# Two-layer attention trunk: last chunk of v moved in the source, one tile more and one exponential buffer fewer

## The chip, the cores and the metric

The kernel runs on one core of one Trainium2 chip. The metric is the device time of one execution in microseconds (us); lower is better. TensorE (PE) multiplies matrices, VectorE (DVE), ScalarE (ACT) and GpSimd (POOL) work on elements, and SyncE (SP) issues most transfers.

## The reference

The input x is 512 positions by 1024 features in float32. There are two layers, each with a mixer and a gated FFN, both with RMS norms ahead and residual sums behind. Layer 0 is stick-breaking attention with 16 heads. Layer 1 is differential attention with 8 heads:

```
q, k, v = split(h @ w_in, 3)          # q, k: 8 heads x 2 maps x 64; v: 8 heads x 128
q, k = rms_norm(q, q_g), rms_norm(k, k_g)       # then rotation of 16 of 64 features
a = softmax(q1 k1) - lam * softmax(q2 k2)       # visible: key chunk <= query chunk (64)
o = rms_norm(a @ v, sub_g) * (1 - lam_init)
x = x + o @ w_out
x = x + (silu(g @ w_gate) * (g @ w_up)) @ w_down    # g = rms_norm(x)
```

## The kernel before

Activations lie transposed, as eight tiles x of 128 features by 512 positions. For accuracy each operand is split into a high and a low part, and each product is three matmuls (mm3, lines 221 to 223). The normalised input h of a mixer is 16 tiles of the tag "t" in the pool hp, a high and a low one for each 128 features. The outputs of the heads (og) take tiles of the same tag, two for each head in layer 1 and two for each pair of heads in layer 0. HP is the number of these tiles, 25. The low part of pair 4 in layer 0, written in line 547, is the 26th tile of the tag in source order, and h still has a reader after it, the last q and k of the layer.

A planner orders the instructions before the kernel runs. It goes by a priority, the place in the source, and by its own estimate of when things are ready; each engine then works through its list in order. Functions under `ahead` (stacks, weights, banks, head_out) are lifted by 200 places. Everything else keeps its place: the filler, that is the projections of later chunks and of the output, which is meant to fill PE between the steps of attention. Each tile is taken from a pool by its tag; a tag has a fixed number of buffers, and the tile waits for a free one.

Layer 1 runs through heads 0 to 7. A chunk c is the pair of heads 2c and 2c + 1. Chunk 0 is projected first. For chunks 1 to 3 two generators are queued in the order qk 1, v 1, qk 2, v 2, qk 3, v 3:

- qk_steps projects q and k for four groups of 128 positions. A group is two steps; at its end line 784 copies the sums to qk_nat, and lines 786 and 787 square and sum them (a tile of the tag tmp each). After the eighth step comes what is left: the reciprocal root of the sums (line 794, then rsqrt, lines 143 to 149, with tiles rs_u and rs_t), the multiplication by it (line 797), and the rotation on GpSimd (lines 814 to 817, two tmp tiles).
- v_steps projects v, one step for each group of positions, with copies in lines 763 and 764.

A head does the following (attend): the weights for the last group of queries, `after()`, a fill, the next weights and two banks of transposes, a fill, `middle()`, weights, a bank and a fill, and again weights, a bank and a fill. A fill pulls as many steps from the queue as `counts` says for this head and place. `after()` is head_out of the head before: it copies the product with v (line 882), transposes and squares it (line 893, a tmp tile), takes the reciprocal root (lines 143 to 149, again rs_u and rs_t), scales, and writes the output to og (lines 918 and 919). `middle()` stacks q and k for the next head (lines 316, 317, 313, 314; the copies of k by line 336 on GpSimd's queue), and for an odd head it first flushes the queue until the next chunk's qk generator is finished. weights() takes scores (lines 342, 343), maxima (841) and exponentials (842) into e1 and e2 and combines them in e1 (854). The bank (368) transposes e1, lines 371 and 372 split it. Before its product with v a head flushes the v generator of its chunk; head 6 then queues out_first, the first half of the output projection (adds in line 289). out_second is the other half (302).

Of the kernel before, what the change touches and what calls it, by code (L numbers as in the profile page):

```python
# [12 lines left out]
F32 = mybir.dt.float32  # L13
# [8 lines left out]
P = 128  # L22
S = 512
# [9 lines left out]
RSQRT_MAGIC = float(0x5F3759DF)  # L33
AHEAD = 200
TCK = dict(schedule_with_timeline_sim=True)
HP = 25
WB = 5
THIRDS = ((0, 8), (8, 8), (16, 6))
TWO_PI_A = 6.28125
# [5 lines left out]
def trunk(  # L45
# [30 lines left out]
    xp = ctx.enter_context(tc.tile_pool(name="xp", bufs=1))  # L76
    hp = ctx.enter_context(tc.tile_pool(name="hp", bufs=HP))
    wp = ctx.enter_context(tc.tile_pool(name="wp", bufs=WB))
# [203 lines left out]
    def out_first(layer, og):  # L282
        for g in range(4):
            w = out_load(layer, 0, g)
            for mi in range(2):
                m = g * 2 + mi
                ps = mm.tile([P, S], F32, tag="mm", name="ps_o")
                out_mms(ps, w, og, range(4), mi, 0, 3)
                V.tensor_tensor(x[m], x[m], ps, op=ALU.add)
                yield  # L290
# [48 lines left out]
    def scores(ps, q2, k2, e, qt):  # L339
        n = max(2, qt + 1) * P  # L340
        qs = slice(qt * P, (qt + 1) * P)
        T.matmul(ps[:, :n], q2[:, e, qs], k2[:, 0, e, :n], start=True, stop=False)
        T.matmul(ps[:, :n], q2[:, e, qs], k2[:, 1, e, :n], start=False, stop=True)
# [391 lines left out]
    def diff_layer(norm, nxt):  # L735
        h = norm.h
        with ExitStack() as st:
# [3 lines left out]
            at = st.enter_context(tc.tile_pool(name="at1", bufs=2))  # L741
# [89 lines left out]
            @ahead  # L831
            def weights(q2, k2, ss, qt):
                n = (qt + 1) * P
                nm = sm.tile([P, 2], F32, tag="nm", name="nm")
                e1 = at.tile([P, S], F32, tag="e1", bufs=5, name="e1")
                e2 = at.tile([P, S], F32, tag="e2", name="e2")
                for e, o in ((0, e1), (1, e2)):
                    ps = scp.tile([P, S], F32, tag="sc", name="sc")
                    scores(ps, q2, k2, e, qt)
                    V.memset(ps[0:64, n - 64 : n], NEG)  # L840
                    V.reduce_max(nm[:, e : e + 1], ps[:, :n], axis=AX.X, negate=True)
                    A.activation(
                        o[:, :n],
                        ps[:, :n],
                        AF.Exp,
                        bias=nm[:, e : e + 1],
                        accum_out=ss[:, e, qt : qt + 1],
                    )
                c = sm.tile([P, 2], F32, tag="c", name="c")
                V.reciprocal(c[:, 0:1], ss[:, 1, qt : qt + 1])  # L850
                V.tensor_scalar(
                    c[:, 1:2], ss[:, 0, qt : qt + 1], nlam, c[:, 0:1], op0=ALU.mult, op1=ALU.mult
                )
                V.scalar_tensor_tensor(
                    e1[:, :n], e2[:, :n], c[:, 1:2], e1[:, :n], op0=ALU.mult, op1=ALU.add
                )
                return e1

            def head(hh, q2, k2, v, after, middle, steps, before):
                ss = sm.tile([P, 2, TT], F32, tag="s12", name="s12")  # L860
                attend(tpp, wts, lambda qt: weights(q2, k2, ss, qt), after, middle, steps)
                before()
                v = v()
                av = avp.tile([P, S], F32, tag="av", name="av")
                hs = slice(hh * P, (hh + 1) * P)
                with tc.high_priority(AHEAD):
                    for kt in range(TT):
                        n, hi, lo = wt_chunk(wts, kt)
                        mm3(
                            av[:, :n],  # L870
                            (v[0][:, kt, hs], v[1][:, kt, hs]),
                            (hi, lo),
                            kt == 0,
                            kt == TT - 1,
                        )
                return av, ss
# [59 lines left out]
                gens["v", c] = v_steps(c, vs)  # L936
                fillers.extend((gens["qk", c], gens["v", c]))
            last = out_first(1, og)
            counts = ((3, 3, 3, 3), (0, 0, 0, 0)) * 3 + ((1, 1, 1, 1), (1, 1, 1, 1))
            for hd in range(8):  # L940
                hh = hd % 2
                c = hd // 2
# [32 lines left out]
    assert not todo  # L975
    n3 = Norm(gf, KT, True, False)
    diff_layer(n2, n3)
    ffn(1, n3, store)

# [72 lines left out]
```

## Time and profile before

| | us |
|---|---|
| median of 3 runs | 1258.3 |
| their range | 1256.72 to 1261.17 |
| profiled execution | 1261.58 |
| its span, first to last instruction | 1259.8 |
| PE busy | 1226.6 |
| DVE busy | 735.3 |

The span is what the trace covers; the time around it is 1.8 us. Layer 0's mixer ends near 260 us, its FFN near 630, layer 1's mixer near 890, and the rest is the second FFN.

### The profile page before, as it was taken

To read this page: it belongs to the slowest core of one execution; us is meant where nothing else is said; L and a number is where in the kernel's file an instruction comes from. 1 tells how busy PE (TensorE), PEld (TensorE's weight loads), DVE (VectorE), ACT (ScalarE), POOL (GpSimd) and SP (SyncE) were. 2 spreads that over 40 slices of the span, in tenths; PEclk is the share of its full clock that TensorE was granted. 3 is DMA by queue.
4 is the path that set the end of the run, shared out by engine and by line. 5 is a ranking of instruction groups with operands and counts; after the bars stand their busy time and mean duration, and the time that the engine had idled before them with its cause. 6 is when DMAs were issued, how large, how long until landed. Compare 5 with 4: busy or idle time off the path is not lost.

```text
span 1259.8 us, 16064 instructions
## 1 busy us (share of the span) xinstructions
PE 1226.6 (97%) x5974; PEld 1023.5 (81%) x5974; DVE 735.3 (58%) x1382; ACT 565.2 (45%) x963; POOL 125.3 (10%) x181
## 2 busy tenths in 40 slices
PE   7899999999999999999999999987999999999998
PEld 6788988878888888888888898766788888888886
DVE  6468788586556555455634686885764344443442
ACT  7687888454334333334424455463543123222320
POOL 2111112041101001111010102100300000000000
PEclk9899999999999999999999999989999999999999
DMA  7955848337767777767736364421333323332322
GB/s 211 219 124 134 197 95 211 69 130 258 245 220 255 248 251 234 247 229 226 278 146 215 97 217 138 164 67 47 105 101 100 100 85 100 100 97 87 97 75 80
DMA packets 58478, 198.40 MB, mean 157 GB/s; under 512 B 8288, under 2 KB 9312, under 8 KB 58400
## 3 DMA queue, kind: packets, MB, share of 16 engines
q1 hardware_dynamic: 41760, 138.90, 34.5%
q0 software_dynamic: 16208, 57.94, 16.5%
q8 instruction: 47, 0.77, 0.2%
q10 hardware_dynamic: 432, 0.53, 0.1%
q14 instruction: 31, 0.25, 0.1%
HBM read 153.31 MB, written 35.65 MB: 150 GB/s over the span
## 4 chain that ended last, share of the span: by engine, by line
PE 90%; DVE 5%; DMA 3%; ACT 2%; issue 1%; SPq 0%; DVEq 0%; ACTq 0%
PE ps_d L223 7%; PE ps_d L222 7%; PE ps_d L221 7%; PE ps_g L222 6%; PE ps_u L223 6%; PE ps_u L222 6%; PE ps_g L223 6%; PE ps_u L221 6%; PE ps_g L221 6%; PE ps_nat L221 4%; PE ps_nat L222 4%; PE ps_nat L223 4%; PE ps_o L221 2%; PE tp L368 2%; PE ps_o L222 2%; PE ps_o L223 2%
## 5 line engine op out<-in xcount | busy, mean ns | idle before, releaser
L110 ACT ACTIVATE whi<-wraw 128x1024 fp32r<-128x1024 f32 (+1 forms) x138 | 140.6, 1033 | 358.9 <-PE ps_d L222 80.5
L111 DVE TENSOR_TENSOR wlo<-wraw,whi 128x1024 fp32r<-128x1024 f32 (+1 forms) x138 | 166.6, 1208 | 101.9 <-ACT whi L110 52.2
L222 PE MATMUL ps_g<-hlo,whi 128*128 128x512 f32 x352 | 138.0, 392 | 1.5 <-DVE hlo L163 1.5
L222 PE MATMUL ps_d<-alo,whi 128*128 128x512 f32 x352 | 138.9, 396 | 0.0
L223 PE MATMUL ps_d<-ahi,wlo 128*128 128x512 f32 x352 | 138.9, 396 | 0.0
L221 PE MATMUL ps_d<-ahi,whi 128*128 128x512 f32 x352 | 138.7, 396 | 0.0
L221 PE MATMUL ps_u<-hhi,whi 128*128 128x512 f32 x352 | 137.2, 390 | 0.5 <-DVE x L302 0.5
L221 PE MATMUL ps_g<-hhi,whi 128*128 128x512 f32 x352 | 137.6, 391 | 0.0
L223 PE MATMUL ps_g<-hhi,wlo 128*128 128x512 f32 x352 | 137.0, 389 | 0.0
L222 PE MATMUL ps_u<-hlo,whi 128*128 128x512 f32 x352 | 137.0, 389 | 0.0
L223 PE MATMUL ps_u<-hhi,wlo 128*128 128x512 f32 x352 | 136.9, 389 | 0.0
L221 PE MATMUL ps_nat<-whi,hhi 128*128 128x256 f32 (+1 forms) x384 | 125.2, 327 | 0.3 <-DVE v L445 0.2
L223 PE MATMUL ps_nat<-whi,hlo 128*128 128x256 f32 (+1 forms) x384 | 124.2, 324 | 0.0
L222 PE MATMUL ps_nat<-wlo,hhi 128*128 128x256 f32 (+1 forms) x384 | 123.7, 323 | 0.0
L620 DVE TENSOR_TENSOR x<-x,ps_d 128x512 f32<-128x512 f32 x48 | 32.7, 684 | 89.5 <-PE ps_d L223 89.5
L222 PEld LDWEIGHTS ps_g<-hlo,whi 128*128 128x128 f32 x352 | 66.1, 188 | 17.2 <-DVE hlo L163 3.2
L221 PEld LDWEIGHTS ps_nat<-whi,hhi 128*128 128x128 f32 x384 | 73.9, 193 | 7.4 <-DVE v L445 1.0
L222 PEld LDWEIGHTS ps_d<-alo,whi 128*128 128x128 f32 x352 | 66.1, 188 | 16.1
L223 PEld LDWEIGHTS ps_d<-ahi,wlo 128*128 128x128 f32 x352 | 66.1, 188 | 16.0
L221 PEld LDWEIGHTS ps_d<-ahi,whi 128*128 128x128 f32 x352 | 66.1, 188 | 15.9
L221 PEld LDWEIGHTS ps_u<-hhi,whi 128*128 128x128 f32 x352 | 66.1, 188 | 14.9 <-DVE x L302 1.3
L223 PEld LDWEIGHTS ps_nat<-whi,hlo 128*128 128x128 f32 x384 | 73.8, 192 | 5.3
(201 smaller groups left out, 2353.7 us busy)
## 6 DMA issues: line engine op xcount, KB each, us to landing
wraw<-in_wgu SPq DMA_DIRECT2D x88, 512.0 KB, 3.5
wraw<-in_wd SPq DMA_DIRECT2D x32, 512.0 KB, 3.6
praw<-in_wqk SPq DMA_DIRECT2D x16, 512.0 KB, 5.8
kept_wqk<-whi POOLq DMA_DIRECT2D x16, 512.0 KB, 5.4
kept_wqk<-wlo POOLq DMA_DIRECT2D x16, 512.0 KB, 6.3
whi<-kept_wqk SPq DMA_DIRECT2D x16, 512.0 KB, 6.1
wlo<-kept_wqk SPq DMA_DIRECT2D x16, 512.0 KB, 5.5
k<-k POOLq DMA_DIRECT2D x30, 256.0 KB, 3.8
```

What stands on the lines that cost most here:

```text
L110: A.activation(hi[:, :cols], raw[:, :cols], AF.Copy)
L111: V.tensor_tensor(lo[:, :cols], raw[:, :cols], hi.bitcast(F32)[:, :cols], op=ALU.subtract)
L221: T.matmul(ps, lh[0], rh[0], start=first, stop=False)
L222: T.matmul(ps, lh[0], rh[1], start=False, stop=False)
L223: T.matmul(ps, lh[1], rh[0], start=False, stop=last)
L368: T.transpose(tp[:, o : o + P], w[qt][:, kt * P : (kt + 1) * P], ident)
L620: V.tensor_tensor(x[m], x[m], ps, op=ALU.add)
```

## The change

Three edits. HP goes from 25 to 26. The tag e1 of the exponentials has 4 buffers in place of 5. In `counts`, the third pair of rows (heads 4 and 5) goes from three steps a fill to two, and the last pair (heads 6 and 7) still pulls one step a fill. So head 4 pulls the eight steps of qk 3 alone; what follows its eighth step is pulled by the flush in the middle of head 5, and the four steps of v 3 by the four fills of head 6, ahead of out_first.

```diff
-HP = 25
+HP = 26
...
-                e1 = at.tile([P, S], F32, tag="e1", bufs=5, name="e1")
+                e1 = at.tile([P, S], F32, tag="e1", bufs=4, name="e1")
...
-            counts = ((3, 3, 3, 3), (0, 0, 0, 0)) * 3 + ((1, 1, 1, 1), (1, 1, 1, 1))
+            counts = ((3, 3, 3, 3), (0, 0, 0, 0)) * 2 + ((2, 2, 2, 2), (0, 0, 0, 0)) + ((1, 1, 1, 1), (1, 1, 1, 1))
```

## Rows read from the trace of the kernel before

**Rows 1.** Busy shares on the page: engine, busy us (share), instructions.

```profile
PE 1226.6 (97%) x5974; PEld 1023.5 (81%) x5974; DVE 735.3 (58%) x1382; ACT 565.2 (45%) x963; POOL 125.3 (10%) x181
```

**Rows 2.** Stretches: length, busy PE, PEld, DVE, ACT, POOL, clock, DMA share, GB/s.

```profile
800.00:830.00 30.00, 28.09 (x139) 22.89 (x137) 22.46 (x66) 12.84 (x38) 5.71 (x10) 0.94 0.35 116
830.00:870.00 40.00, 33.28 (x169) 26.19 (x167) 29.75 (x109) 21.31 (x65) 1.18 (x2) 0.91 0.13 32
870.00:890.00 20.00, 14.90 (x57) 11.34 (x55) 10.66 (x24) 8.50 (x19) 1.54 (x2) 0.83 0.26 74
```

**Rows 3.** Timeline of GpSimd, 800 to 832: start, duration, engine, line, out<-in.

```profile
803.78 0.45 POOL L814 TENSOR_TENSOR rope<-qk_nat,rot 128x128 f32<-128x128 f32 x1 [14.85 <-DVE qk_nat L797]
...
806.80 1.47 POOL L817 TENSOR_TENSOR qk_nat<-rope 128x256 f32<-128x256 f32 x2
826.96 0.60 POOL L336 DMA_DIRECT2D k<-k  x1 [18.68 <-DVE c L850]
828.72 0.61 POOL L336 DMA_DIRECT2D k<-k  x1 [1.16 <-DVE rs_t L148]
```

**Rows 4.** Timeline of PE: head 4's last transpose, scores of head 6, head 6's last bank.

```profile
813.24 0.27 PE L368 MATMUL tp<-ident,e 128*128 128x128 f32 x1
...
830.16 0.47 PE L342 MATMUL sc<-k,q 128*128 128x512 f32 x1
...
831.76 0.47 PE L342 MATMUL sc<-k,q 128*128 128x512 f32 x1 [0.47 <-DMA k<-k]
...
846.73 0.90 PE L368 MATMUL tp<-ident,e 128*128 128x128 f32 x3 [0.31 <-DVE wt_lo L372]
```

**Rows 5.** Stretches, the matmuls into ps_nat alone: length, busy PE, clock, DMA share, GB/s.

```profile
780.00:800.00 20.00, 10.99 (x81) 1.00 0.83 273
800.00:830.00 30.00, 0.00 (x0) 0.94 0.35 116
```

**Rows 6.** Timeline of ScalarE: copies and squares of chunks 2 and 3.

```profile
729.52 0.69 ACT L784 ACTIVATE qk_nat<-ps_nat,rstd 128x512 f32<-128x512 f32 x1 [0.27 <-PE ps_nat L223]
...
741.53 0.37 ACT L893 ACTIVATE o_sq<-tn,rs 128x128 f32<-128x128 f32 x1
...
741.87 1.16 ACT L786 ACTIVATE qk_sq<-qk_nat 128x512 f32<-128x512 f32 x2
...
776.87 0.69 ACT L784 ACTIVATE qk_nat<-ps_nat,rstd 128x512 f32<-128x512 f32 x1 [3.10 <-PE ps_nat L223]
...
789.37 0.39 ACT L893 ACTIVATE o_sq<-tn,rs 128x128 f32<-128x128 f32 x1
...
789.71 1.18 ACT L786 ACTIVATE qk_sq<-qk_nat 128x512 f32<-128x512 f32 x2
```

**Rows 7.** Timeline of VectorE: ending of chunk 3, head 4's last weights, head 4's root.

```profile
796.05 0.17 DVE L143 TENSOR_SCALAR rs_u<-qk_ss 128x32 int32<-128x32 int32 x1
...
801.34 2.29 DVE L797 TENSOR_TENSOR qk_nat<-qk_nat,rs_u 128x2048 f32<-128x2048 f32 x1
...
807.32 0.36 DVE L854 SCALAR_TENSOR_TENSOR e<-e,c,e 128x128 f32<-128x128 f32 x1
...
826.58 0.15 DVE L143 TENSOR_SCALAR rs_u<-o_ss 128x4 int32<-128x4 int32 x1
```

**Rows 8.** Timeline of ScalarE: stacks of heads 5 and 6, product of head 5, exponential.

```profile
778.58 0.68 ACT L316 ACTIVATE q<-tqk,gqT 64x512 fp32r<-64x512 f32 x1 [0.53 <-PE tqk L827]
...
825.26 0.58 ACT L313 ACTIVATE k<-tqk 64x512 fp32r<-64x512 f32 x1
...
835.69 0.59 ACT L882 ACTIVATE wraw<-av 128x512 f32<-128x512 f32 x1
...
845.98 0.68 ACT L842 ACTIVATE e<-sc,nm 128x512 f32<-128x512 f32 x1
```

**Rows 9.** Timeline of ScalarE and VectorE in layer 0: output of pair 4.

```profile
185.36 0.64 ACT L546 ACTIVATE ohi<-o 128x512 fp32r<-128x512 f32 x1
...
194.59 0.67 DVE L547 TENSOR_TENSOR olo<-o,ohi 128x512 fp32r<-128x512 f32 x1
```

## The prediction, made before the changed kernel ran

> **What bounds the kernel now.** I read the busy shares first. TensorE (PE) is busy 97% of the span [rows 1], so over the whole kernel only about 33 us are not matmul time. The table by stretches then shows where part of these lie in layer 1: from 800 to 890 us PE is busy 28.09 of 30, 33.28 of 40 and 14.90 of 20 us, while VectorE (DVE) has 22.46, 29.75 and 10.66 [rows 2]. That is 13.7 us without a matmul in 90, and the mean granted clock falls to 0.94, 0.91 and 0.83 of full speed, a mix of the 1.2 and 2.4 GHz levels [rows 2]. In this end of the attention little is left to fill PE with, and a chain sets the time: stacks of q and k, scores, exponentials, weights, output of heads 5, 6 and 7. The timelines then show what holds head 6. Its two k transfers are issued on GpSimd's queue at 826.96 and 828.72, its first scores run at 830.16, and the second ones, at 831.76, name the transfer as what they waited for [rows 3, 4]. So head 6's start is bound by its stacks, these by the last chunk of q and k (its normalisation and rotation, called its ending here), and the end of the layer, with the FFN behind it, by heads 6 and 7.
>
> **What the change does to v.** v3, the last chunk of v, is 96 matmuls. Projections of q, k and v take 10.99 us of PE between 780 and 800 and nothing from 800 to 830 [rows 5]. So v3, traced in head 4, is done by 800, though its first reader is head 6's product with v. The planner does not place filler where the source yields it, but once PE is free and the data are there. The change traces v3 in head 6: still behind the last q and k chunk, still ahead of out_first, its four weight loads still ahead of out_first's on the SyncE queue, and attention still ahead of it by the same priority of 200. Nothing that it reads or writes comes later, so I expect v3 to run before 800 as now: price 0, and its copies (0.5 us each on ScalarE and DVE) stay where they are. If it did move, its 10.99 us could fill at most the 13.7 us of gaps; that is a rival below.
>
> **What it does to the ending of qk3.** This edit I price. With (3,3,3,3) head 4 pulled twelve steps: eight of qk3, then its ending, then v3. With (2,2,2,2) it pulls the eight alone. The ending is then traced by the flush in head 5's middle, after head 5 has called head_out for head 4. It uses the tags rs_u, rs_t and tmp, and so does head_out. The trace shows that tiles of one tag are granted in source order, whoever is ready first. The squares of chunk 2 had all their data by 730.2; they ran at 741.87, right behind the last output square of head 1 (741.53), which stands just ahead of them in the source. Those of chunk 3 had theirs by 777.6 and ran at 789.71, behind head 3's last one (789.37) [rows 6]. ScalarE sat idle for 3.10 us before the fourth copy of chunk 3, with squares of earlier copies outstanding [rows 6]. So the ending must now wait until head_out of head 4 has taken its root tiles: 826.58 in this trace, where today the ending's own root starts at 796.05 [rows 7]. Attention of heads 4 and 5 goes on meanwhile on DVE; behind the ending wait the rotation and, on GpSimd's queue, the k transfers of heads 6 and 7, and nothing else.
>
> **The sum.** From the ending's root to head 6's first scores it takes 34.1 us today (796.05 to 830.16): 5.3 for the root, 2.3 for the multiplication, 4.6 for the rotation, then stacks and transfer [rows 3, 4, 7].
> - Upper bound: the gate stays at 826.58 and the path takes 34.1 again. Head 6 starts at 860.7, 30.5 late.
> - Lower bound: head 4 ends sooner, since the ending no longer stands ahead of its last exponentials on DVE. That is 2.29 + 11 x 0.17 = 4.2 us. PE also let head 4's last transposed weights wait from 807.68 to 813.24, 5.6 us [rows 4, 7]. Without both the gate opens at 816.8. The shortest path is a root of 1.9 (11 x 0.17), 2.3, 4.6, q in 3.4 (transposes 0.6, four copies of 0.7, as that at 778.58), k transposes 0.6, and 4.9 from the first k copy to the scores (825.26 to 830.16): 17.7 us [rows 3, 4, 7, 8]. Head 6 starts at 834.5, 4.3 late.
> - My value: the gate at 819.6 (all of the 4.2, half of the 5.6) and a path of 24.0, nearer to the short end, because the 34.1 holds waits behind filler on PE, and PE has gaps by then [rows 2]. Head 6 starts at 843.6, 13.4 late.
>
> Not all of this reaches the end. After head 6's first scores head 5 still used the engines for 5.5 us, until its product was copied out at 835.69 [rows 4, 8]; starting late, head 6 runs alone. I take back 5 of that (0 to 5.5). This leaves 8.4, between 0 and 30. More idle PE may cost more at the lower clock level, as in the three stretches [rows 2]; the upper bound holds that.
>
> **The buffers.** One exponential buffer fewer: a head's four weights are live until its last bank is transposed, so the next head's first exponential must follow the first of those transposes. Head 7's ran at 845.98; the transposes of head 6 began at 846.73 and take 0.3 each, so it would come 1.1 us later [rows 4, 8]. On head 7's path that is 0 to 1.1; I take 0.6. Up to head 3 full PE covers it; without that cover each head would pay up to the same 1.1. One tile more for h and outputs: in layer 0 the low part of pair 4 came at 194.59, 9.2 us after its high part at 185.36 [rows 9]. Counted in the source it is the 26th tile of its tag and waited for an h tile. With 26 it comes at once, but its reader is the second half of the projection, after the last head: 0. In layer 1 head 4's output comes past 826.58, after v3 has freed h: 0 too.
>
> A rule would have this otherwise. The Trainium skill, Perfetto Trace Analysis, section Optimization Strategy under Identifying Performance Opportunities, says that a gap repeating on the engine that should be saturated can mean too little memory for the next tile. By it the h tile could be worth those 9.2 us, and the sum would fall to 1258. The trace bears it out only in part: the late tile is there, but it is a DVE result on which PE does not wait.
>
> Sum: 8.4 + 0.6 = 9.0 us on the profiled 1261.6, which lies 3.3 above the median of the runs. That gives 1270.6 there and **1267** as a median.
>
> **Rivals.**
> - The ending comes late but is hidden, or grants are looser than I read them. At the lower bound the 4.3 is eaten by the 5 taken back: 1258. For it: 4.8 us pass today between the rotation's end (808.27) and the next transposes of q (near 813), which can shrink. Against: head 6 starts the moment its k lands.
> - On the other side, the ending leaves DVE to head 4. If head 4 finishes so early that the gate opens before 812.5 (830.16 less 17.7), head 6 starts sooner than today and the 4.2 us saved on head 4's chain are kept: 1254. This needs 14.1 us from head 4, of which the rows show 9.8.
> - v3 does move into head 6 and half of its 10.99 us fill gaps: 1258.3 - 5.5 = 1253. Against: filler runs when ready [rows 5].
> - The h tile lifts a stall in layer 0: 1258.3 - 9.2 = 1249. Against: its only readers come after the last head.
>
> **How the numbers follow.** Late ending, slower: 0.60, its own range 1262 to 1282. Hidden or no change: 0.21. Early gate 0.10, v3 moved 0.06, h tile 0.03. A measurement of this kernel can tell about 0.3%, 3.8 us, from no change; so faster 0.19, same 0.21, slower 0.60. The range 1254 to 1279 leaves out the far side of the faster rivals and the top of the upper bound, under 2 in 10 together.
>
> **What the next profile would show.** Right: qk3's multiplication only after head 4's root has begun, the rotation ending past 824, head 6's first scores past 835 with a PE gap ahead of them; v3 still before 800; head 7's first exponential behind head 6's last transposes; in layer 0 pair 4's low part some 1 us behind its high part. Wrong: that multiplication still near 801, which would mean that grants are not in source order; v3 matmuls past 830; head 4's product copied out before 808.

## The result, and the profile after

The changed kernel takes 1267.44 us (median of four executions, 1266.91 to 1268.62) against 1258.43 us for the kernel before (four executions). The ratio is 1.0077, 95% interval 1.0063 to 1.0092: slower by 9.0 us, outside the 0.3% that the prediction takes as the least it can tell. The forecast was 1267.0 us, slower. The profiled execution took 1268.62 us, 7.0 over that of before.

The page's busy shares of the changed kernel have the same count of instructions on every engine as [rows 1]; PE is busy 3.6 us longer:

```profile
PE 1230.2 (97%) x5974; PEld 1024.7 (81%) x5974; DVE 738.2 (58%) x1382; ACT 565.3 (45%) x963; POOL 125.2 (10%) x181
```

The three stretches of [rows 2], in the changed kernel:

```profile
800.00:830.00 30.00, 26.71 (x130) 22.06 (x128) 21.06 (x73) 9.52 (x32) 0.04 (x1) 0.96 0.29 104
830.00:870.00 40.00, 28.33 (x101) 20.24 (x99) 26.16 (x79) 19.54 (x53) 6.81 (x12) 0.65 0.12 26
870.00:890.00 20.00, 18.26 (x90) 14.62 (x91) 11.37 (x45) 7.62 (x26) 0.00 (x0) 1.00 0.21 65
```

The middle stretch is the one that changed: 101 matmuls where [rows 2] have 169, 11.7 us without any, and a mean granted clock of 0.65, so most of it at 1.2 GHz. GpSimd's work (POOL) has moved out of the first stretch into it.

The stretches of the matmuls into ps_nat, as in [rows 5]: v3 is still done before 800 (its last matmul starts at 789.88).

```profile
780.00:800.00 20.00, 7.25 (x56) 6.96 (x56) 1.91 (x4) 1.90 (x4) 1.00 0.64 183
800.00:830.00 30.00, 0.00 (x0) 0.00 (x0) 0.00 (x0) 0.00 (x0) 0.96 0.29 104
```

VectorE's timeline after, against [rows 7]. The ending's root (128x32) starts in the slot behind the root of head 4 (128x4), at 824.26 where it was 796.05:

```profile
824.10 0.16 DVE L143 TENSOR_SCALAR rs_u<-o_ss 128x4 int32<-128x4 int32 x1
...
824.26 0.15 DVE L143 TENSOR_SCALAR rs_u<-qk_ss 128x32 int32<-128x32 int32 x1
...
827.49 2.29 DVE L797 TENSOR_TENSOR qk_nat<-qk_nat,rs_u 128x2048 f32<-128x2048 f32 x1
```

GpSimd's timeline after, against [rows 3]: the rotation ends at 834.4, and the k transfers of head 6 follow at 841.01 and 842.36.

```profile
829.96 0.45 POOL L814 TENSOR_TENSOR rope<-qk_nat,rot 128x128 f32<-128x128 f32 x1 [40.22 <-DVE qk_nat L797]
...
833.00 1.42 POOL L817 TENSOR_TENSOR qk_nat<-rope 128x256 f32<-128x256 f32 x2
841.01 0.60 POOL L336 DMA_DIRECT2D k<-k  x1 [6.59 <-DVE k L314]
842.36 0.61 POOL L336 DMA_DIRECT2D k<-k  x1 [0.74 <-DVE k L314]
```

PE's timeline after, against [rows 4]: transposes of the stacks (tqk), a gap of 3.48 us ahead of the second group, head 6's first scores at 845.69 in place of 830.16, and much later head 6's last bank.

```profile
834.21 0.60 PE L827 MATMUL tqk<-ident,qk_nat 128*128 128x128 f32 x4
838.29 1.09 PE L827 MATMUL tqk<-ident,qk_nat 128*128 128x128 f32 x4 [3.48 <-DVE q L317]
...
845.69 0.63 PE L342 MATMUL sc<-k,q 128*128 128x512 f32 x1
...
860.50 1.11 PE L368 MATMUL tp<-ident,e 128*128 128x128 f32 x4 [1.17 <-DVE wt_lo L372]
```

ScalarE's timeline after: the second exponential of head 7 waits for these transposes, the sign of an e1 buffer being set free. (The first one, at 859.86, waits for nothing of the kind. The reciprocal of line 850 at 860.67 takes its sum, so it is the one into e2.)

```profile
861.02 0.69 ACT L842 ACTIVATE e<-sc,nm 128x512 f32<-128x512 f32 x1 [0.38 <-PE tp L368]
```

### The profile page after: what moved, and what is told of

Its sections match the earlier page's. It is cut to its first block, busy times and chain, and to the rows that moved or that the text cites. A ratio compares the mean times of both kernels' runs of the same rounds, so it can differ in the third digit from the quotient of the medians.

```text
span 1266.8 us, 16060 instructions
## 1 busy us (share of the span) xinstructions
PE 1230.2 (97%) x5974; PEld 1024.7 (81%) x5974; DVE 738.2 (58%) x1382; ACT 565.3 (45%) x963; POOL 125.2 (10%) x181
## 4 chain that ended last, share of the span: by engine, by line
PE 90%; DVE 4%; ACT 2%; DMA 2%; issue 1%; SPq 0%; DVEq 0%; ACTq 0%
PE ps_d L223 6%; PE ps_d L222 6%; PE ps_d L221 6%; PE ps_g L222 6%; PE ps_u L222 6%; PE ps_u L223 6%; PE ps_g L223 6%; PE ps_u L221 6%; PE ps_g L221 6%; PE ps_nat L221 4%; PE ps_nat L222 4%; PE ps_nat L223 4%; PE ps_o L221 2%; PE ps_o L222 2%; PE ps_o L223 2%; PE tp L368 2%
## 5 line engine op out<-in xcount | busy, mean ns | idle before, releaser
L221 PEld LDWEIGHTS ps_g<-hhi,whi 128*128 128x128 f32 x352 | 66.1, 188 | 14.4 <-issue 0.5
```

The lines of the kernel that those rows point to most:

```text
L221: T.matmul(ps, lh[0], rh[0], start=first, stop=False)
```

## Experiments

Layer 1's first exponential stands at 679.6 to 684.7 us in these profiles, and the kernel before and e1_six, whose lists are nearly the same, are 2.4 us apart there. So the table counts from that instruction, in each kernel's own profile, in us. "Last bank" is the start of head 7's last transposes of weights, "product" the copy of its product with v, "second transposes" those of its output (tb), "FFN" the first matmul into ps_g. The ratio and its interval come from executions of the kernel and of the one before on the same chip. A profiled execution can lie up to 4 us off the median (before 1261.58, e1_three 1274.07), so differences of 2 or 3 us against these two rows carry little.

| kernel | e1 buffers | ending's root | head 6's first exponential | last bank | product | second transposes | FFN | ratio |
|---|---|---|---|---|---|---|---|---|
| before | 5 | 111.4 | 148.0 | 177.1 | 184.6 | 193.5 | 205.0 | 1 |
| after | 4 | 143.1 | 166.9 | 192.5 | 196.5 | 206.1 | 215.1 | 1.0077 (1.0063 to 1.0092) |
| counts_only | 5 | 134.3 | 158.6 | 187.5 | 195.5 | 204.4 | 216.8 | 1.0082 (1.0068 to 1.0096) |
| buffers_only | 4 | 112.2 | 149.1 | 175.4 | 179.5 | 189.3 | 198.3 | 0.9956 (0.9943 to 0.9968) |
| ending_in_head4 | 4 | 113.1 | 150.0 | 176.2 | 180.2 | 189.9 | 198.9 | 0.9961 (0.9948 to 0.9973) |
| own_root_and_rope | 4 | 112.2 | 148.0 | 179.4 | 183.4 | 193.0 | 202.1 | 0.9983 (0.9974 to 0.9993) |
| own_root | 4 | 112.2 | 160.6 | 187.2 | 191.2 | 200.9 | 209.9 | 1.0064 (1.0052 to 1.0076) |
| e1_four | 4 | 112.2 | 149.1 | 175.4 | 179.4 | 189.0 | 198.0 | 0.9966 (0.9953 to 0.9979) |
| e1_six | 6 | 111.4 | 146.6 | 174.7 | 182.2 | 191.0 | 202.7 | 1.0001 (0.9992 to 1.0011) |
| own_all_before | 4 | 113.6 | 149.9 | 177.1 | 181.1 | 190.7 | 199.8 | 0.9973 (0.9963 to 0.9984) |
| tmp_two | 5 | 111.8 | 146.5 | 176.6 | 180.6 | 190.3 | 199.3 | 0.9958 (0.9944 to 0.9972) |
| e1_three | 3 | 119.3 | 158.1 | 190.4 | 197.5 | 206.4 | 218.1 | 1.0106 (1.0089 to 1.0123) |
| last_out_in_tn | 5 | 111.4 | 148.0 | 176.1 | 181.5 | 190.4 | 203.4 | 1.0008 (0.9997 to 1.0019) |

### The two halves of the change

counts_only is the kernel before with the last line of the diff alone:

```diff
-            counts = ((3, 3, 3, 3), (0, 0, 0, 0)) * 3 + ((1, 1, 1, 1), (1, 1, 1, 1))
+            counts = ((3, 3, 3, 3), (0, 0, 0, 0)) * 2 + ((2, 2, 2, 2), (0, 0, 0, 0)) + ((1, 1, 1, 1), (1, 1, 1, 1))
```

> Edit: only the new counts, with 25 tiles for h and outputs and 5 exponential buffers as before. Theory (the ending of qk chunk 3 is granted its root and rotation tiles only after head 4's output stage): nearly the whole loss is here, 1264 to 1269, with the multiplication of chunk 3 at 827 or later and head 6's first scores near 845. Rival (the loss comes from the exponential buffer): 1257 to 1260 and the scores of head 6 near 830.

Measured: 1268.33 us, 10.8 over the kernel before on that chip (1257.52). The new counts alone are as slow as the whole change. Two of the marks came sooner than expected, the multiplication at 821.48 and head 6's first scores at 838.57, since head 4's root comes at 816.57 here; the ending's own root still follows it, by 0.31 us.

buffers_only is the kernel before with the other two edits:

```diff
-HP = 25
+HP = 26
...
-                e1 = at.tile([P, S], F32, tag="e1", bufs=5, name="e1")
+                e1 = at.tile([P, S], F32, tag="e1", bufs=4, name="e1")
```

> Edit: 26 tiles for h and outputs and 4 exponential buffers, with the counts as before. Theory: 1257 to 1261, the multiplication of chunk 3 near 801, head 6's first scores near 830, and in layer 0 pair 4's low part 1 us behind its high part. Rival (the exponential buffer): 1264 to 1269 with late first exponentials of each head. Rival (the h tile lifts a stall in layer 0): 1249 to 1254.

Measured: 1252.31 us, 5.2 below the kernel before. A gain where the forecast has a loss of 0.6: the first surprise. The multiplication of chunk 3 is early (796.75), as expected, but the time lies below the range, in that of the rival with the h tile; e1_four, further down, rules this rival out. In layer 0 the low part of pair 4 does come soon behind its high part (181.23 on ScalarE), 2.1 us after it in place of the 9.2 of [rows 9], as this row of VectorE's timeline of buffers_only shows:

```profile
183.35 0.69 DVE L547 TENSOR_TENSOR olo<-o,ohi 128x512 fp32r<-128x512 f32 x1
```

### The ending put back, v3 left where the change puts it

ending_in_head4 is the changed kernel, with the rest of qk3 pulled before head 4's product:

```diff
                 def before():
+                    if hd == 4:
+                        flush(gens["qk", 3])
```

> Edit: the changed kernel, but the ending of qk chunk 3 is pulled at the end of head 4, ahead of head 4's output stage in the source; v3 stays in head 6. Theory: the loss goes, 1256 to 1262, the multiplication of chunk 3 before 806. Rival (v3's later place in the source, with its lower rank on PE, costs the time): 1264 to 1269, although the ending runs early.

Measured: 1252.45 us, the same as buffers_only (1252.31). So v3's later place costs nothing, and the whole loss hangs on the ending (its multiplication is back at 799.14): 5.1 us below the kernel before with it early, 9.0 above with it late, 14.1 us in all.

### What holds the ending: two tags and the order of the list

In own_root_and_rope and own_root the ending of chunk 3 gets a tile of its own, in the changed kernel with HP at 25. own_root takes it for rs_u and rs_t alone, own_root_and_rope for the rotation's tmp tile too:

```diff
-                u = rsqrt(ss, 32)
+                own = qp.tile([P, S], F32, tag="own", bufs=1, name="own") if c == 3 else None
+                u = rsqrt(ss, 32, own)
...
-                    mt = tmp.tile([P, S], F32, tag="tmp", name="rope")
+                    mt = own if own is not None else tmp.tile([P, S], F32, tag="tmp", name="rope")
```

> Edit: the changed kernel with the ending still traced in head 5, but its root and rotation use one tile of a tag of their own, paid for by going back to 25 tiles for h and outputs. Theory (grants of one tag in source order are the cause, not the ending's rank): the ending runs ahead of head 4's root, its multiplication before 812, and the time falls to 1256 to 1263. Rival (the ending's lower rank on VectorE is the cause, since attention of heads 5 and 6 now stands ahead of it): multiplication still past 820, 1264 to 1269.

Measured: 1255.66 us. The ending's root is back at 112.2 and head 6's first exponential at 148.0, though the source has the ending behind head 4's output as in the changed kernel. Waiting for tiles that head 4's output takes was the cause. Of the 14.1 us it returns 11; head 7's last bank comes 3 us later than in ending_in_head4 (179.4 against 176.2), although head 6 starts 2 us sooner, which I did not follow up.

> Edit: the changed kernel, the root tiles of chunk 3's ending have a tag of their own, but its rotation still uses the shared tag tmp; 25 tiles for h and outputs. Theory (each shared tag is granted in source order): the multiplication runs at 796 to 806, but the rotation on GpSimd not before head 4's output squares, 818 or later, ending near 825; head 6's first scores near 837 and the time between the two, 1258 to 1265. Rival (only the root tiles gate): rotation right behind the multiplication, 1253 to 1258.

Measured: 1265.03 us. The root is early, head 6 is not. But the rotation did not wait on the chip. GpSimd's timeline of own_root has it at 803.64, done by 808.4:

```profile
803.64 0.45 POOL L818 TENSOR_TENSOR rope<-qk_nat,rot 128x128 f32<-128x128 f32 x1 [11.01 <-DVE c L854]
...
806.87 1.49 POOL L821 TENSOR_TENSOR qk_nat<-rope 128x256 f32<-128x256 f32 x2
```

PE's timeline of the same kernel has the transposes that read it 21.6 us later, behind those of head 4's output (tn), with no wait named for them:

```profile
825.85 0.60 PE L892 MATMUL tn<-ident,wraw 128*128 128x128 f32 x4
...
830.00 0.60 PE L831 MATMUL tqk<-ident,qk_nat 128*128 128x128 f32 x4
```

In own_root_and_rope PE's timeline has them within 3 us of the end of the rotation (805.9):

```profile
808.10 0.60 PE L831 MATMUL tqk<-ident,qk_nat 128*128 128x128 f32 x4
```

On the chip the tile was free long before, so it is not there that the tag does its work. What is left is the planner: as I read it, the rotation waits there for its tmp tile, and the transposes get their late place in PE's list, to which PE keeps. (The planner's own reckoning is not on record.) The expectation that the rotation itself would be seen late was wrong.

own_all_before is the kernel before with four e1 buffers, where squares, root and rotation of every chunk use tiles of a tag of their own:

```diff
-                    sq = tmp.tile([P, S], F32, tag="tmp", name="qk_sq")
+                    sq = qp.tile([P, S], F32, tag="own", bufs=1, name="qk_sq")
...
-                u = rsqrt(ss, 32)
+                own = qp.tile([P, S], F32, tag="own", bufs=1, name="own")
+                u = rsqrt(ss, 32, own)
...
-                    mt = tmp.tile([P, S], F32, tag="tmp", name="rope")
+                    mt = own if own is not None else tmp.tile([P, S], F32, tag="tmp", name="rope")
```

> Edit: the kernel before with 4 exponential buffers, and squares, root and rotation of all chunks of q and k on one tile of a tag of their own. Theory: chunk 3's squares no longer wait for head 3's output squares and run before 782, its rotation ends before 795; since with 4 buffers head 6 no longer waits for its stacks, there is no further gain: within 3 us of the run with 4 buffers. Rival (head 6 still waits for its stacks): 4 us or more below that run.

Measured: 1254.40 us, against 1252.78 for e1_four. The time is within the theory's 3 us, but not by the theory's steps: of chunk 3's four squares three still run behind head 3's output squares, the ending's root stands at 793.97 (794.08 in e1_four), and the rotation ends at 806.3. ScalarE's timeline of own_all_before:

```profile
759.35 0.62 ACT L789 ACTIVATE qk_sq<-qk_nat 128x512 f32<-128x512 f32 x1
...
785.85 0.39 ACT L897 ACTIVATE o_sq<-tn,rs 128x128 f32<-128x128 f32 x1
...
786.97 0.63 ACT L789 ACTIVATE qk_sq<-qk_nat 128x512 f32<-128x512 f32 x1
```

So a tile of its own did not bring the ending forward here, and what an earlier ending would be worth in the old order stays open. With one tile for all four squares, each of them also has to wait until the one before is summed on VectorE, the first only at 784.54: the squares' late place need not come from the tag that they share with head 3's output.

### Where the gain of four buffers comes from

e1_four and e1_six are the kernel before with four and with six e1 buffers:

```diff
e1_four
-                e1 = at.tile([P, S], F32, tag="e1", bufs=5, name="e1")
+                e1 = at.tile([P, S], F32, tag="e1", bufs=4, name="e1")
e1_six
-HP = 25
+HP = 24
...
-                e1 = at.tile([P, S], F32, tag="e1", bufs=5, name="e1")
+                e1 = at.tile([P, S], F32, tag="e1", bufs=6, name="e1")
```

> Edit: only the exponential buffers go from 5 to 4; 25 tiles for h and outputs and the old counts stay. Theory (the fewer buffers hold the next head's first exponential back until the head before is transposed, so that heads 5, 6 and 7 run one after the other and PE keeps its clock; the gain of both buffer edits together, ratio 0.9956, is theirs): 1251 to 1255, the pairs of a head's exponentials under 2 us apart, as in the run with both. Rival (the h tile gives the gain): 1256 to 1260, the exponentials as in the kernel before.

> Edit: 6 exponential buffers, paid for with one tile for h and outputs fewer (24); old counts. Theory (exponential buffers let the next head run ahead into the one before): no better than with 5, 1256 to 1264, the first exponential of head 5 before head 4's last bank. Rival (the planner's order shifts with any edit and the gain of four buffers is chance): anything from 1250 to 1268, with no relation between the number of buffers and how far heads overlap.

Measured: 1252.78 and 1257.53 us (before: 1256.94). Four alone give the gain, so the tile for h and outputs gives none that can be told (0.9956 against 0.9966, intervals overlapping), and a sixth buffer changes nothing. The table says where the gain is: up to the last bank e1_four is no sooner than e1_six (175.4 and 174.7), but from there to the FFN it takes 22.6 us in place of 28.0. So the gain is not in keeping the heads apart, as the expectation had it. PE's timeline of e1_six from the last bank on:

```profile
857.00 0.66 PE L368 MATMUL tp<-ident,e 128*128 128x128 f32 x4 [0.45 <-DVE wt_lo L372]
...
862.32 0.39 PE L221 MATMUL av<-wt_hi,v1h 128*128 128x512 f32 x1
...
866.33 0.60 PE L888 MATMUL tn<-ident,wraw 128*128 128x128 f32 x4
...
873.33 1.08 PE L915 MATMUL tb<-ident,wraw 128*128 128x128 f32 x4 [4.32 <-DVE wraw L906]
875.19 0.80 PE L221 MATMUL ps_o<-ohi,whi 128*128 128x512 f32 x1 [0.78 <-ACT ohi L918]
```

Between 857.4 and 862.5 stand 21 matmuls of the output projection, ahead of the product (av); 18 more follow it, and then PE has nothing for 4.32 us, until head 7's output is scaled. The kernel before does the same (product from 867.1, gap of 4.32 at 878.13). The same stretch in e1_four:

```profile
857.26 0.60 PE L368 MATMUL tp<-ident,e 128*128 128x128 f32 x4
858.55 0.50 PE L221 MATMUL av<-wt_hi,v1h 128*128 128x512 f32 x1 [0.69 <-ACT wt_hi L371]
...
862.88 0.60 PE L888 MATMUL tn<-ident,wraw 128*128 128x128 f32 x4
870.87 0.63 PE L915 MATMUL tb<-ident,wraw 128*128 128x128 f32 x4
872.27 0.50 PE L221 MATMUL ps_o<-ohi,whi 128*128 128x512 f32 x1 [0.78 <-ACT ohi L918]
```

None of that filler stands between bank and product, and it covers all of the wait for the output. Three more kernels test whether this place of the filler, and not the number of buffers, is the gain. Their edits:

```diff
tmp_two
-    tmp = ctx.enter_context(tc.tile_pool(name="tmp", bufs=3))
+    tmp = ctx.enter_context(tc.tile_pool(name="tmp", bufs=2))
e1_three
-                e1 = at.tile([P, S], F32, tag="e1", bufs=5, name="e1")
+                e1 = at.tile([P, S], F32, tag="e1", bufs=3, name="e1")
last_out_in_tn
-                after = partial(head_out, av, ss, *((tnp, "tn") if hd < 7 else (tqp, "tq")))
+                after = partial(head_out, av, ss, *((tnp, "tn") if hd < 9 else (tqp, "tq")))
```

> The kernel before with the pool of squares, roots' neighbours and rotations (tag tmp) cut from three buffers to two; five exponential buffers as before. In PE's list this moves the filler of the output projection: 6 matmuls instead of 21 stand ahead of the last head's product, and the rest stands behind it. Theory: what four exponential buffers gained is this place of the filler at the layer's end, not the buffers: no idle PE ahead of the last head's second transposes (4.3 us in the kernel before), last bank to first FFN matmul about 22.7 us in place of 28.0, ratio about 0.9966 of the kernel before, 1252.5 us. Rival: the gain needs four exponential buffers, through shorter heads: with five it stays at 1.000, or over it for the scarcer tmp tiles.

Measured: 1252.49 us, ratio 0.9958, with five e1 buffers; 22.7 us from last bank to FFN. As the theory has it; the 6 matmuls of the expectation stand ahead of the last bank, none between it and the product. PE's timeline of tmp_two:

```profile
857.58 0.60 PE L368 MATMUL tp<-ident,e 128*128 128x128 f32 x4
858.87 0.50 PE L221 MATMUL av<-wt_hi,v1h 128*128 128x512 f32 x1 [0.69 <-ACT wt_hi L371]
...
871.32 0.63 PE L915 MATMUL tb<-ident,wraw 128*128 128x128 f32 x4
```

> The kernel before with three exponential buffers in place of five. In PE's list the filler stands ahead of the last head's product as in the kernel before (17 matmuls behind the last bank). Theory (the place of the filler decides): the idle stretch of about 4.3 us is there again, so none of the gain of four buffers, and the heads lose some 0.6 to 3 us more for the scarcer buffers: ratio 1.000 to 1.003. Rival (fewer buffers keep the heads apart, and that is the gain): as fast as four or faster, 0.9966 or below.

Measured: 1270.39 us, ratio 1.0106. The gap of 4.31 us is back and the end takes 27.7 us, so the rival falls; but I had the heads' loss far too small, with the ending's root 7.9 us late. (Here the last bank is torn apart: three of its transposes start at 187.5, the last at 190.4, and the table and the 27.7 go by this one. It comes 12.9 us after the last transpose of the kernel before.) PE's timeline of e1_three:

```profile
873.92 0.27 PE L368 MATMUL tp<-ident,e 128*128 128x128 f32 x1
...
889.83 1.08 PE L915 MATMUL tb<-ident,wraw 128*128 128x128 f32 x4 [4.31 <-DVE wraw L906]
```

> The kernel before, with the transposes of the last head's output in the same PSUM bank (tn) as those of the other heads, so that one part of the filler (9 matmuls), which takes that bank, must wait until the last head's output is out. 8 matmuls in place of 17 stand between the last bank and the last product, and the 9 come behind the second transposes. Theory: the product comes 2.1 us sooner, but PE has just as much idle time (about 4.3 us), since nothing is added between the product and the second transposes: ratio 0.999 to 1.001. Rival (the product's own lateness is the cost): 2.1 us faster, 0.9983.

Measured: 1259.08 us, ratio 1.0008. The product comes 7.5 us after the last bank in the kernel before and 5.4 us after it here, the gap stays at 4.32, and the time is the same. The product's lateness alone is no cost; the idle PE is. (The 17 and 8 matmuls of two of these expectations are 21 and 12 in the traces.) PE's timeline of last_out_in_tn:

```profile
862.27 0.39 PE L221 MATMUL av<-wt_hi,v1h 128*128 128x512 f32 x1
...
873.27 1.09 PE L915 MATMUL tb<-ident,wraw 128*128 128x128 f32 x4 [4.32 <-DVE wraw L906]
```

All thirteen kernels fall into two groups by this place. The eight with no filler between the last bank and the product take 22.6 to 22.9 us from the last bank to the FFN; the other five take 27.3 to 29.3, with a gap of 4.3 to 4.4. No edit moves the filler alone, since each one can change the rest of the lists too; the case for its place as the cause is this agreement.

## Why the prediction came true, and what in it did not

The total was right to 0.4 us, but two of its terms were off in opposite directions, so that closeness is luck. What was right is the direction, and what holds the ending.

**v3: right.** It runs before 800 in the changed kernel, and ending_in_head4 shows that its place in the source is worth nothing.

**What holds the ending: right, with one refinement.** It follows head 4's root by 0.16 us, and own_root_and_rope undoes that by tiles alone. own_root adds that, for the rotation, the grant in source order is not a wait on the chip; what the chip sees of it is the order in an engine's list. The squares of [rows 6], from which the prediction read this rule, do not show it by themselves: in own_all_before three of four stay behind head 3's output squares without sharing a tag with them.

**The gate and the path: right for the counts alone.** I had head 4's root 7.0 us sooner than in the kernel before (819.6 for 826.58). With five buffers (counts_only) it stands at 134.0 after the first exponential, where the kernel before has 141.9: 7.9 sooner. With four buffers it stands at 142.9, head 4's product being copied 8.9 us later (817.04 in the changed kernel, 135.9 after the first exponential, against 127.0 in counts_only): the two edits meet at this gate, and I had priced them one by one. The path of 24.0 measured 21.4 (824.26 to 845.69) in the changed kernel and 21.7 in counts_only.

**"I take back 5": wrong.** From head 6's first exponential to head 7's product it takes 29.6 us in the changed kernel and 30.2 in ending_in_head4, although head 5 is out of the way in the former. Head 6 starts 16.9 us later and the FFN 16.2 later. With five buffers it is the same: in counts_only head 6 starts 10.6 us later than in the kernel before (13.4 in the prediction), and the FFN 11.8 later. Nearly all of the lateness reaches the end. So the term of 8.4 measured 10.8 (counts_only) and, with four buffers, 14.1 us.

**The buffers: wrong in sign.** The step that failed is "On head 7's path that is 0 to 1.1". The wait is there, though at head 7's second exponential and not its first (861.02, behind the transposes of 860.50), and up to the last bank four buffers gain nothing. But I looked at the heads alone and left out a gain without a reason: another buffer count gives PE another list, and in it the filler stands elsewhere. The term of +0.6 measured -4.2 (e1_four), and -1.8 beside the late ending (9.0 less 10.8, not to be told from 0 by the intervals). There the end gains too (22.6 us from the last bank to the FFN, 29.3 in counts_only), but the later gate takes most of it back (last bank at 192.5, 187.5 in counts_only). The row that could have told it was in the trace of the kernel before: 4.32 us of idle PE ahead of head 7's second transposes, behind filler that had run ahead of the product. PE's timeline of the kernel before:

```profile
861.81 0.65 PE L368 MATMUL tp<-ident,e 128*128 128x128 f32 x4 [0.44 <-DVE wt_lo L372]
...
867.12 0.39 PE L221 MATMUL av<-wt_hi,v1h 128*128 128x512 f32 x1
...
878.13 1.09 PE L915 MATMUL tb<-ident,wraw 128*128 128x128 f32 x4 [4.32 <-DVE wraw L906]
```

I had counted it in the 14.90 of 20 us of [rows 2] and put it down to the chain.

**The tile for h: right,** and with it the doubt about the rule on repeating gaps (the Trainium skill, Perfetto Trace Analysis, Optimization Strategy under Identifying Performance Opportunities: they can mean too little memory for the next tile). The h tile bought no time that can be told. The gap at the layer's end, a single one, is not such a repeating gap: it went away with less memory, one e1 or one tmp tile fewer, and stayed with one e1 tile more (and one h tile fewer) or two e1 tiles fewer.

**Still open:** what in the planner's estimate puts the filler ahead of the product with three, five and six e1 buffers and behind it with four, or with two tmp tiles. And whether both gains add: the best of these kernels (0.9956 to 0.9966) agree within their intervals. And what an earlier ending would be worth in the old order, which own_all_before did not bring about.

## What to carry to other kernels

In a kernel whose instruction order a planner writes, an edit of a buffer count can be an edit of every engine's list: look at what the list puts ahead of the last chain of each stage before pricing the wait itself. Work that could cover a wait is worth more behind the start of the chain than ahead of it, and an idle stretch right behind filler is a sign that it may stand on the wrong side. And a tag shared by two chains can tie them even where the chip never waits for the tile, so a step that is moved in the source should be checked for the tags that it shares with what it now follows.

## What the hardware showed beside this

Here an idle stretch slowed the matmuls behind it as well. The stretches of e1_six around the gap (filler and product, the idle 4.3 us, the last filler) show the granted clock at 1.00 before and 0.76 behind it, part of that at 1.2 GHz:

```profile
862.30:869.00 6.70, 6.70 (x35) 5.38 (x33) 0.46 (x3) 2.63 (x10) 0.00 (x0) 1.00 0.00 0
869.00:873.30 4.30, 0.01 (x1) 0.01 (x1) 3.69 (x14) 0.42 (x1) 0.00 (x0) 0.96 0.36 71
875.10:885.10 10.00, 9.91 (x34) 7.88 (x34) 6.40 (x8) 5.28 (x10) 1.41 (x2) 0.76 0.30 88
```

The last filler of tmp_two, without the gap ahead of it:

```profile
872.70:880.50 7.80, 7.77 (x34) 6.30 (x34) 6.15 (x8) 5.17 (x8) 1.34 (x2) 1.00 0.32 77
```

The same 34 matmuls take 9.91 and 7.77 us, 2.1 us more behind the gap. From the last bank to the FFN PE is idle for 5.1 us in e1_six and for 1.7 in e1_four; these 3.4 us and the 2.1 together are about the 5.4 between 28.0 and 22.6. And the four transposes of a group, 0.60 us in most of these rows, took 1.09 in the changed kernel's stretch at 0.65.
